# Softmax with a temperature: the first store issued ahead of two exponentials

## Chip, cores, metric

One core of one Trainium2 chip. The metric is the device time of one execution in microseconds (us); less is better.

## The reference

```python
# x: 16 x 1024 x 512, float32
x_scaled = x / 0.5
x_max = np.max(x_scaled, axis=-1, keepdims=True)
exp_x = np.exp(x_scaled - x_max)
return exp_x / np.sum(exp_x, axis=-1, keepdims=True)
```

The input is 33.55 MB and so is the output. Every byte is read once and written once.

## The kernel before

The 16,384 rows form eight tiles of 128 partitions x 16 rows x 512 elements, 4.19 MB each. Tiles 0 to 5 have a buffer of their own; tile 6 reuses tile 0's and tile 7 reuses tile 1's. SyncE issues the loads. VectorE takes the row maxima (`shift`), ScalarE the exponentials with their sums, in place. Then VectorE scales seven eighths of the rows and ScalarE the last eighth (of a block of only four rows VectorE scales all). ScalarE also issues the stores, one for each tile.

```python
    LOADS = [[(0, 4), (4, G)]] + [WHOLE] * 7
    BLOCKS = [[(0, 4), (4, 8), (8, G)]] + [WHOLE] * 6 + [[(0, 8), (8, G)]]
    STORES = [WHOLE] * 8
    BUFS = 6
    ...
    def exponentials(i):
        ...
        for g in range(hi - lo):
            row = chunks[c][:, lo + g, :]
            nc.scalar.activation(out=row, in_=row, func=EXP, bias=..., scale=2.0,
                                 accum_out=sums[i][:, g : g + 1])
    ...
    shift(0)
    shift(1)
    exponentials(0)
    for i in range(n):
        if i + 1 < n:
            exponentials(i + 1)
        scale_vector(i)
        scale_scalar(i)
        if i + 2 < n:
            shift(i + 2)
        store(i)
```

A block i is a tile or a part of one. Tile 0 is cut into blocks 0, 1 and 2, so tile 0's store comes in round i = 2, after all sixteen exponentials of block 3, which is tile 1.

## Time and profile before

| | before |
|---|---|
| time, median of the first 3 runs | 162.47 us (162.2 to 162.55) |
| span of the profiled run | 160.6 us |
| VectorE (DVE) busy | 134.6 us, 84% |
| ScalarE (ACT) busy | 102.1 us, 64% |
| bytes moved | 67.13 MB, 418 GB/s over the span |
| first store issued / landed | 45.58 / 69.3 us |
| last store issued / landed | 147.55 / 159.7 us |

The span is what the profiler sees; the time is some 1.7 us longer. A transfer has "landed" when all its bytes have arrived and those who wait for it are told. Two readings of the profile compete: that VectorE is the bound, and that the transfers (DMA) are.

This line is from the view of waits of the kernel before (engine, what it waited for, total us, times, longest):

```profile
DVE negmax L74 <- DMA xt<-in_x_dram: 9.5, 2, 4.8
```

VectorE waits for loads twice, and both times for the two pieces of tile 0. After 12.88 us it never waits for a load again.

### The profile page before, as it was taken

How to read it: one execution, taken by the hardware profiler on the slowest of the kernel's cores; microseconds unless marked ns; L12 is line 12 of the kernel's file. 1: busy time of each engine (PE TensorE's matmuls, PEld its weight loads, DVE VectorE, ACT ScalarE, POOL GpSimd, SP SyncE). 2: the span in 40 equal slices, each digit the busy share in tenths (PEclk: the TensorE clock that was granted, in tenths of full speed). 3: DMA queues.
4: the chain of work that ended last, by engine and by line, in shares of the span. 5: the costliest groups of instructions: out<-in, count | busy, mean ns of one | idle time of the engine just before them, and what ended most of it. 6: DMA issues, size and time to landing. Idle time of an engine off the chain costs nothing.

```text
span 160.6 us, 402 instructions
## 1 busy us (share of the span) xinstructions
DVE 134.6 (84%) x45; ACT 102.1 (64%) x273; POOL 0.2 (0%) x4
## 2 busy tenths in 40 slices
DVE  0507999999999999999999999999999999957000
ACT  3071549069979963998199909991899891790000
POOL 0000000000000000000000000000000000000000
DMA  5999999999999999999999999999999999999993
GB/s 182 471 400 506 400 400 498 408 392 484 424 400 384 400 457 449 400 441 465 400 424 473 408 408 492 400 392 498 416 392 490 424 392 457 457 392 449 465 392 139
DMA packets 2450, 67.13 MB, mean 418 GB/s; under 512 B 272, under 2 KB 272, under 8 KB 272
## 3 DMA queue, kind: packets, MB, share of 16 engines
q1 hardware_dynamic: 1296, 33.56, 49.3%
q10 hardware_dynamic: 1152, 33.55, 48.4%
q14 instruction: 2, 0.02, 0.0%
HBM read 33.55 MB, written 33.55 MB: 418 GB/s over the span
## 4 chain that ended last, share of the span: by engine, by line
DVE 80%; DMA 7%; ACT 4%; issue 0%; SPq 0%
DVE negmax L74 42%; DVE xt L102 36%; DMA xt<-in_x_dram 7%; ACT xt L85 4%; DVE bias L78 1%; DVE recip L100 1%; SPq L66 0%
## 5 line engine op out<-in xcount | busy, mean ns | idle before, releaser
L85 ACT ACTIVATE xt<-xt,bias 128x512 f32<-128x512 f32 x128 | 90.4, 708 | 41.7 <-DVE bias L78 41.2
L74 DVE TENSOR_REDUCE negmax<-xt 128x16 f32<-128x8192 f32 (+2 forms) x11 | 69.9, 6352 | 9.5 <-DMA xt<-in_x_dram 9.5
L102 DVE TENSOR_TENSOR xt<-xt,recip 128x7168 f32<-128x7168 f32 (+2 forms) x11 | 62.0, 5637 | 0.4
L85 ACT ACTIVATION_READ_ACCUMULATOR xt<-xt,bias 128x1 f32 x128 | 23.9, 187 | 0.0
L111 ACT ACTIVATE xt<-xt,recip 128x512 f32<-128x512 f32 x15 | 9.9, 706 | 0.0
L100 DVE RECIPROCAL recip<-sums 128x16 f32<-128x16 f32 (+2 forms) x11 | 2.4, 218 | 1.8 <-ACT xt L85 1.8
L78 DVE TENSOR_SCALAR bias<-negmax 128x16 f32<-128x16 f32 (+2 forms) x11 | 1.9, 173 | 0.4
L52 ACT ACT_TABLE_LOAD x1 | 1.3, 1283 | 0.7 <-PEq L148 0.7
L51 DVE MEMSET warm<- 128x1 f32 x1 | 0.1, 59 | 0.8 <-PEq L148 0.8
L52 ACT ACTIVATE warm<-warm 128x1 f32<-128x1 f32 x1 | 0.2, 203 | 0.0
L148 POOL MEMSET const-bfloat16-1.0<- 128x1 bf16 x1 | 0.1, 103 | 0.0
L148 POOL MEMSET const-uint8-127<- 128x1 uint8 x1 | 0.1, 103 | 0.0
L148 POOL MEMSET const-float32-1.0<- 128x1 f32 x1 | 0.1, 100 | 0.0
L148 POOL MEMSET const-float32-0.0<- 128x1 f32 x1 | 0.1, 99 | 0.2 <-issue 0.2
## 6 DMA issues: line engine op xcount, KB each, us to landing
out_dram<-xt ACTq DMA_DIRECT2D x8, 4096.0 KB, 22.8
xt<-in_x_dram SPq DMA_DIRECT2D x7, 4096.0 KB, 30.2
xt<-in_x_dram SPq DMA_DIRECT2D x1, 3072.0 KB, 11.7
xt<-in_x_dram SPq DMA_DIRECT2D x1, 1024.0 KB, 4.9
```

What stands on the lines that cost most here:

```text
L51: nc.vector.memset(warm, 0.0)
L52: nc.scalar.activation(out=warm, in_=warm, func=EXP)
L74: nc.vector.tensor_reduce(negmax[:, 0:b], chunks[c][:, lo:hi, :], axis=AX, op=MAX, negate=True)
L78: nc.vector.tensor_scalar_mul(biases[i][:, 0:b], negmax[:, 0:b], 2.0)
L85: nc.scalar.activation(out=row, in_=row, func=EXP, bias=biases[i][:, g : g + 1], scale=2.0, accum_out=sums[i][:, g : g + 1],)
L100: nc.vector.reciprocal(recips[i][:, 0:b], sums[i][:, 0:b])
L102: nc.vector.tensor_mul(rows, rows, recips[i][:, 0:k].unsqueeze(2).broadcast_to((P, k, D)))
L111: nc.scalar.activation(out=row, in_=row, func=COPY, scale=recips[i][:, g : g + 1])
L148: nc = _bacc.Bacc("TRN2", target_bir_lowering=False, num_devices=1)
```

## The change

The intent is to get the first store going sooner: two of tile 1's exponentials don't have to run before it, so they are put behind it. Nothing is added or removed.

```diff
-    def exponentials(i):
+    def exponentials(i, rows):
         c, lo, hi = blocks[i]
-        sums[i] = stats.tile([P, BMAX], fp32, name="sums")
-        for g in range(hi - lo):
+        if i not in sums:
+            sums[i] = stats.tile([P, BMAX], fp32, name="sums")
+        for g in rows:
...
-    exponentials(0)
+
+    def rows(i):
+        c, lo, hi = blocks[i]
+        cut = hi - lo - (2 if c == 1 else 0)
+        return range(cut), range(cut, hi - lo)
+
+    exponentials(0, rows(0)[0])
     for i in range(n):
         if i + 1 < n:
-            exponentials(i + 1)
+            exponentials(i + 1, rows(i + 1)[0])
         scale_vector(i)
         scale_scalar(i)
         if i + 2 < n:
             shift(i + 2)
         store(i)
+        if i + 1 < n:
+            exponentials(i + 1, rows(i + 1)[1])
```

## The prediction

> **What bounds the kernel now.** I read the page first for the busy shares, then the chain of waits, then the DMA queues, because the first two point at VectorE and the third does not.
>
> ```profile
> span 160.6 us, 402 instructions
> ...
> DVE 134.6 (84%) x45; ACT 102.1 (64%) x273; POOL 0.2 (0%) x4
> ...
> DMA  5999999999999999999999999999999999999993
> ...
> HBM read 33.55 MB, written 33.55 MB: 418 GB/s over the span
> ...
> DVE 80%; DMA 7%; ACT 4%; issue 0%; SPq 0%
> ```
>
> The chain (last line) makes VectorE the bound: it runs from one instruction to the next from 12.88 us to 147.48 us. But it ends 13 us before the span does, and what fills these 13 us is the last store. The DMA row has a 9 in every slice but the first and the last. So I cut the span into stretches to see the rate. The columns are the stretch, its length, the busy time of three engines, the clock, the DMA share and GB/s.
>
> ```profile
> 0.00:3.00 3.00, 0.06 (x1) 1.49 (x2) 0.20 (x4) 1.00 0.40 98
> 3.00:43.00 40.00, 32.37 (x15) 21.05 (x59) 0.00 (x0) 1.00 1.02 438
> 43.00:55.00 12.00, 11.93 (x5) 11.16 (x32) 0.00 (x0) 1.00 0.98 396
> 55.00:95.00 40.00, 39.86 (x9) 29.23 (x78) 0.00 (x0) 1.00 1.00 433
> 95.00:135.00 40.00, 39.79 (x13) 32.20 (x86) 0.00 (x0) 1.00 1.00 432
> ```
>
> The rate is 432 to 438 GB/s with loads alone (3 to 43 us), with loads and stores mixed (55 to 95 us) and later, when stores soon run alone. Only the stretch around the first store is lower. So the time is a sum of bytes: 67.13 MB / 433 GB/s = 155.0 us; the start costs 3 us x (1 - 98/433) = 2.3 us; the dip at the first store costs 12 us x (1 - 396/433) = 1.0 us. That is 158.3 us. The last store lands at 147.55 + 12.2 = 159.75 us (issue time and time to landing), so some 1.4 us remain for smaller losses and the confirmation of the last bytes; the span ends at 160.6 us and the time of that run was 162.34 us, 1.7 us more.
>
> Is the last store late because VectorE finished late? The store before it was issued at 133.08 us and took 17.0 us, so it landed at 150.1 us, 2.5 us after the last store was already in the queue. From landing to landing is 9.65 us, which is 4.19 MB at 434 GB/s: the queue drains at its full rate, with a backlog. VectorE and the DMA engines finish nearly together, with the DMA behind. Both need looking at.
>
> **What the Trainium skill says.** "DMA: Bandwidth & Descriptors", section "Issuing engines are not separate DMA queues": transfers started by different engines run on the same 16 DMA engines and interleave. The trace agrees: with both queues filled the sum stays at 433 GB/s. The same page, "Where 436 GB/s comes from", puts the ceiling of these 16 engines at 435 GB/s; the 432 to 438 measured here (a stretch counts whole packets, hence more than the ceiling) lies on it. "Perfetto Trace Analysis", "Identifying the Most-Contended Engine": what counts is the most contended resource, and for DMA the bandwidth reached instead of occupancy. That is why I set the rate above the chain of waits here.
>
> **The change part by part.** The compiled order of ScalarE shows one difference: the first copy (the row scaled on ScalarE) and the first store stand after 30 exponentials instead of 32, and the last two exponentials of tile 1 follow the store. The order on VectorE and SyncE is the same. Nothing is added or removed, so no byte and no instruction changes; three things move.
>
> Here is that spot in the timeline before (start, duration, instruction):
>
> ```profile
> 43.43 0.71 ACT L85 ACTIVATE xt<-xt,bias 128x512 f32<-128x512 f32 x1
> ...
> 44.14 0.71 ACT L85 ACTIVATE xt<-xt,bias 128x512 f32<-128x512 f32 x1
> 44.75 0.19 ACT L85 ACTIVATION_READ_ACCUMULATOR xt<-xt,bias 128x1 f32 x1
> 44.84 0.71 ACT L111 ACTIVATE xt<-xt,recip 128x512 f32<-128x512 f32 x1
> 45.58 0.37 ACTq L119 DMA_DIRECT2D out_dram<-xt  x1
> 46.18 0.17 DVE L78 TENSOR_SCALAR bias<-negmax 128x16 f32<-128x16 f32 x1
> 46.26 0.25 DVE L100 RECIPROCAL recip<-sums 128x16 f32<-128x16 f32 x1
> 46.39 0.72 ACT L85 ACTIVATE xt<-xt,bias 128x512 f32<-128x512 f32 x1 [0.84 <-DVE bias L78]
> ```
>
> 1. *The store.* Exponentials follow each other every 0.705 us, so two are 1.41 us. The copy starts at 43.43 and the store at 45.58 - 1.41 = 44.17 us. Nothing else holds the store back: VectorE's scaling of tile 0 ends at 37.55 us. The gain for this one store is 1.4 us at its issue.
>
> 2. *What the store feeds.* The load of tile 6 reuses tile 0's buffer and is issued when this store has landed: at 45.58 + 23.7 = 69.3 us before (SyncE issues it at 69.38 us). After, up to 1.4 us sooner. But that load takes 25.6 us and lands at 95.0 us, and VectorE only asks for tile 6 at 104.03 us. So the earlier load removes a wait that does not exist: there is no VectorE wait on a load after 12.88 us (two waits, 9.5 us in all, both on tile 0). And the DMA engines are not idle beside it either: load 5 is in flight until about 3.8 + 71.8 = 75.6 us (issue and time to landing). The store moves ahead of other bytes, and those move behind it. Loads of tiles 4 and 5 may land up to 1.4 us later; tile 5 is asked for at 87.41 us, so about 12 us are spare. Value of this part: 0.0 us.
>
> 3. *The two exponentials.* They now end after the store's issue: 44.17 + 0.37 + about 0.03 gives 44.57, the second starts at 45.27, its accumulator read ends 0.80 us later, at 46.07 us. VectorE's reciprocal needs these sums and started at 46.26 us behind its own bias instruction. So 0.2 us are spare. If ScalarE needs a few tenths more to restart after the issue than I put in, the reciprocal slips by 0.1 to 0.3 us and the whole rest of VectorE's chain with it. The next exponential waits for the bias of 46.35 us anyway, so ScalarE loses nothing.
>
> Would a slip of 0.1 to 0.3 us count? In the packet records behind the page the last store's first packet starts at 148.44 us, right when the first engine ends the store before; 15 of the 16 engines take it up between 148.4 and 148.9 us, the slowest one at 149.6 us, and it is the slowest that ends the span. A slip of up to about 1 us is hidden behind that one.
>
> Sum: store 1.4 us earlier, all hidden behind a full DMA; 0.0 to +0.1 us at the end. The span stays at 160.6 us, the time at the 162.2 to 162.55 us of before.
>
> **The rivals.**
>
> *A: the dip belongs to where the store begins.* Around the first store the rate drops to 396 GB/s, worth 1.0 us. If that came from the store meeting the load of tile 4 at a bad moment, an earlier issue could make it smaller or larger. For: it is the only place in the middle of the span where DMA time is lost. Against: the store moves by 1.4 us inside the same two queued loads (tiles 4 and 5), so the circumstances are the same; I expect the same dip 1.4 us earlier. If it vanished: 161.4 us; VectorE's chain would then be about as late as the DMA, so no more than that. If it grew by half: 162.9 us.
>
> *B: the intent comes true.* The store starts the stream of writes, and 1.4 us earlier would carry through to the end if the DMA engines were starved between 45 and 148 us: 161.0 us. Against: the share is 0.98 to 1.02 in every stretch from 3 to 135 us; a start 1.4 us sooner can't use time that is in use.
>
> *C: VectorE becomes the bound.* The late sums (part 3) push VectorE's chain. With a slip of 0.3 us the last store is issued at 147.85 us and the end is unchanged; only a slip above 1 us shows, and then by the rest. A restart cost of over 1 us on ScalarE isn't in the trace of any place. If it were: 162.7 us.
>
> **Range and chances.** The main case, no change, has about 85% and gives 162.2 to 162.6 us, the spread of the three runs before. A takes about 10%, mostly between 161.5 and 162.9 us; B and C the rest. I predict 162.4 us, and 161.9 to 162.9 us holds the main case with the milder forms of A and C. Two per cent would be 3.2 us; none of the rivals reaches it, so I put 0.98 on within 2% and 0.01 on either side.
>
> **What would show each step.** The first store should start at 44.2 us. The two exponentials behind it should begin near 44.6 us and the reciprocal of tile 1 near 46.3 us; at 46.6 us or later C is at work. The load of tile 6 should be issued 0.7 to 1.4 us before 69.38 us, and no VectorE wait on a load should be new. The rate should be 432 to 438 GB/s outside the dip, the dip again about 1 us, only sooner. The last store should land within 0.3 us of 159.75 us. I am wrong if the time leaves 161.9 to 162.9 us: below it, the dip has gone (look at the rate from 43 to 55 us) or the DMA had idle time that I did not see; above it, the last store was issued more than 1 us later, or the dip grew.

## The result

The changed kernel took 162.20 us (median of 4 runs, 162.04 to 162.22), the kernel before 162.33 us (4 runs, 162.06 to 162.55). The ratio is 0.999 with a 95% interval of 0.9972 to 1.0009: the same. A ratio here is the mean time of one kernel's runs over that of the other's of the same rounds, so it isn't quite the ratio of the medians.

First the spot that was changed, in the timeline of the kernel after (start, duration, instruction):

```profile
43.38 0.70 ACT L112 ACTIVATE xt<-xt,recip 128x512 f32<-128x512 f32 x1
44.11 0.38 ACTq L120 DMA_DIRECT2D out_dram<-xt  x1
44.53 0.72 ACT L86 ACTIVATE xt<-xt,bias 128x512 f32<-128x512 f32 x1 [0.45 <-ACT xt L112]
...
45.87 0.19 ACT L86 ACTIVATION_READ_ACCUMULATOR xt<-xt,bias 128x1 f32 x1
46.12 0.17 DVE L78 TENSOR_SCALAR bias<-negmax 128x16 f32<-128x16 f32 x1
46.20 0.24 DVE L101 RECIPROCAL recip<-sums 128x16 f32<-128x16 f32 x1
```

The store starts 1.47 us sooner than before; 0.06 us of this are of the whole trace, in which VectorE is earlier by as much. The exponentials behind it start 0.04 us after it was issued. Their sums are ready at 46.06 us, and the reciprocal still comes right behind its own bias instruction, as before. So VectorE lost nothing.

Then the load that this store sets free, in SyncE's timeline after:

```profile
68.16 0.33 SPq L66 DMA_DIRECT2D xt<-in_x_dram  x1
```

It is issued 1.22 us sooner than the 69.38 us of before. But it takes 27.7 us to land instead of 25.6, so it lands at 95.9 us, 0.9 us later than before. The store took DMA time from the loads in flight: tiles 4 and 5 land 0.9 us later too (57.2 and 76.6 us instead of 56.3 and 75.6), and tiles 6 and 7 stand behind them in the same queue. So an earlier store made every later load later. VectorE doesn't notice, since the line of the waits view is unchanged:

```profile
DVE negmax L74 <- DMA xt<-in_x_dram: 9.5, 2, 4.8
```

Last the rates, from the table of stretches after (stretch, length, busy time of three engines, clock, DMA share, GB/s):

```profile
3.00:43.00 40.00, 32.43 (x15) 21.11 (x59) 0.00 (x0) 1.00 1.01 437
43.00:55.00 12.00, 11.93 (x5) 11.27 (x32) 0.00 (x0) 1.00 0.98 396
55.00:95.00 40.00, 39.86 (x9) 29.17 (x78) 0.00 (x0) 1.00 1.00 433
95.00:135.00 40.00, 39.79 (x13) 32.20 (x86) 0.00 (x0) 1.00 1.00 433
```

They are those of before within 1 GB/s, the 396 of the dip included. The last store is issued at 147.50 us and lands 11.9 us later, at 159.4 us. That is 0.3 us sooner than before; in e11 below, the same kernel, it is 159.95 us.

### The profile page after: what moved, and what is told of

It reads as the page before. It is cut to its first block, busy times and chain, and to the rows that moved or that the text cites. A ratio compares the mean times of both kernels' runs of the same rounds, so it can differ in the third digit from the quotient of the medians.

```text
span 160.3 us, 402 instructions
## 1 busy us (share of the span) xinstructions
DVE 134.6 (84%) x45; ACT 102.2 (64%) x273; POOL 0.2 (0%) x4
## 2 busy tenths in 40 slices
DMA packets 2450, 67.13 MB, mean 419 GB/s; under 512 B 272, under 2 KB 272, under 8 KB 272
## 4 chain that ended last, share of the span: by engine, by line
DVE 80%; DMA 7%; ACT 4%; issue 0%; SPq 0%
DVE negmax L74 42%; DVE xt L103 36%; DMA xt<-in_x_dram 7%; ACT xt L86 4%; DVE bias L78 1%; DVE recip L101 1%; SPq L66 0%
```

## The experiments

My theory was: the DMA engines are full from 3 us on, so an earlier store only changes places with loads. Its rivals were that the store's start carries through to the end, that VectorE alone is the bound, and that the dip at the first store depends on where the store stands. Twelve runs were made; e11 is the changed kernel itself.

A word on one measure: most packets of 32 KB took 1213 ns in the packet records of the trace, whatever the mix of loads and stores. The dip consists of load packets that took up to 2 us (up to 3.3 us in e11). I added up what the packets took beyond that pace, for each place, as a mean over the 16 engines, in the one profiled run of each kernel:

| kernel | first store issued | excess at the first store | excess at later stores |
|---|---|---|---|
| before | 45.58 us | 0.76 us | none |
| after | 44.11 us | 0.75 us | none |
| e11, the same kernel again | 44.24 us | 1.0 us | none |
| e10, four exponentials behind | 42.70 us | 0.91 us | none |
| e12, six | 41.17 us | 0.97 us | none |
| e1, eight | 40.00 us | 1.05 us | 0.64 us |

The excess at the first store seems to rise with the shift, but this is not shown: the same kernel has 0.75 us in one run and 1.0 us in another.

### The changed kernel again, and other distances (e11, e10, e12, e1)

```diff
-        cut = hi - lo - (2 if c == 1 else 0)
+        cut = hi - lo - (4 if c == 1 else 0)   # e10; e12 has 6, e1 has 8, e11 keeps 2
```

Expected for e11:

> The changed kernel itself once more, in more rounds and on the same chip as e10. Theory 'full DMA': ratio to the kernel before 1.000 within 0.002. If the 0.13 us between the medians of the first comparison is an effect of the change, the ratio is 0.999 again with an interval that leaves 1.000 out.

Measured: 162.21 us, ratio 1.0000 (0.9988 to 1.0013). The interval holds 1.000, so no effect is shown. The medians do lie 0.10 us apart in the same direction again; so small a difference can't be told from noise here.

Expected for e1, the first of them to run:

> The changed kernel with eight exponentials of tile 1 behind the first store instead of two. The store should be issued 8 x 0.705 = 5.6 us before the 45.58 us of the kernel before, near 39.9 us, and tile 1's reciprocal stay near 46.2 us. Theory 'the 16 DMA engines are full, the store only changes places with loads': ratio 1.000 within 0.003, the dip in the rate 5.6 us sooner and still worth about 0.8 us. Rival 'the stream of writes starts sooner and carries through': 5.6 us less, ratio 0.966. Rival 'the dip belongs to the place where the store meets the loads': the dip's loss changes by half or more, time by 0.4 us or more.

Measured: 163.38 us, ratio 1.0065 (1.005 to 1.0081). The store did start 5.6 us sooner and VectorE's reciprocal did stay (46.32 us), so the rival of the carried-through start is refuted. But my own theory's 1.000 missed too: the kernel is 1.1 us slower. The same stretches of the kernel before, then of e1:

```profile
62.00:68.00 6.00, 5.93 (x4) 4.99 (x15) 0.00 (x0) 1.00 1.00 431
...
81.00:87.00 6.00, 6.00 (x1) 6.00 (x19) 0.00 (x0) 1.00 1.00 431
```

```profile
62.00:68.00 6.00, 5.93 (x4) 4.94 (x14) 0.00 (x0) 1.00 0.98 410
...
81.00:87.00 6.00, 6.00 (x1) 6.00 (x19) 0.00 (x0) 1.00 1.00 404
```

At the starts of the second and third store, near 64 and 84 us, load packets are long again, which they are not in the kernel before. With the third of these places, near 103 us, the excess is the 0.64 us of the table, and with the larger first dip some 0.9 us more than before (part of that first dip may be the scatter between runs). The last store was issued at 147.83 us and took 12.9 us, so it landed 1.0 us after the 159.7 us of before. So the sum of bytes has a second term, the pace of the packets, and this term can depend on where stores start. Two runs asked what it depends on.

e1 also shows the price that the loads pay. The load of tile 7 landed at 115.05 us before, 5.5 us ahead of VectorE; in e1 it landed at 120.81 us, and VectorE waited 0.15 us for it, too short to be counted in the view of waits. Tile 6, which the prediction looked at, had 9 us. This does not explain the 1.1 us: the last store was issued only 0.28 us later and then stood longer in the queue than before. But with a longer shift VectorE's chain would wait too.

Expected for e10:

> The changed kernel with four exponentials behind the first store: issue near 42.8 us. e1 (eight, 39.9 us) was 0.65% slower with two further stretches of long load packets, at the starts of the second and the third store. If this grows with the shift, this run loses about 0.4 us: ratio 1.002 to 1.004. If it comes only where the 16 engines start a store far apart in time (2.5 us in e1, about 1 us before), the time follows the spread at the starts of the second and third store: ratio 1.000 with a spread near 1 us, 1.004 to 1.007 with 2.4 us.

Expected for e12:

> The changed kernel with six exponentials behind the first store: issue near 41.4 us, between e10 (42.8 us, ratio 1.000) and e1 (39.9 us, ratio 1.0065). The load of tile 4 has its first packets near 41.1 us in all of them, so only e1 issues the store while tile 3 is still the one being loaded. If the loss grows with the shift: ratio 1.003 to 1.005. If it is tied to that tile boundary: ratio 1.000, within 0.002, with no long load packets at the starts of the second and third store. In both cases nothing is gained.

Measured: e10 162.26 us, ratio 0.9998 (0.9984 to 1.0011); e12 162.32 us, ratio 0.9997 (0.9983 to 1.0011). Neither has long packets at later stores. So the loss in time does not grow steadily with the shift: between 1.5 and 4.4 us early it is absent, at 5.6 us it is there. One idea fell here: that it comes when the 16 engines start a store far apart in time. In e1 they ended the first store, and so came to the second, 2.3 us apart, and 0.9 us before; but in the profiled runs of e12 and e11 they were 2.0 and 2.8 us apart, without a stretch of long packets there. The other idea is weak: in e1 alone the store is clearly issued before the packets of tile 4, which start at 41.1 us (e12's is issued at 41.17 us, on the boundary itself). One kernel on one side of a boundary is thin evidence, I have no mechanism for it, and e2 below has long packets at a later store too, though its first store comes late. This stays open.

### The first store late (e2, e3)

```diff
+        if i == 3:          # e3: i == 4
+            store(2)
-        store(i)
+        if i != 2:
+            store(i)
```

Expected for e2:

> The kernel before with the first store held back until just ahead of the second, near 59.0 us, 13.4 us late. Theory 'full DMA': six loads of 4.19 MB at 433 GB/s fill the engines from 1.8 us to about 60.5 us by themselves, so nothing idles and the time stays: ratio 1.000 within 0.005; the load of tile 6 goes out near 71 us instead of 69.4 us. Rival 'the first store's issue time carries through to the end': 13 us more, ratio 1.08.

Measured: 162.67 us, ratio 1.0022 (1.0007 to 1.0036). The time stayed within the forecast, but not the issue time, which was 54.17 us and not 59.0:

```profile
54.17 0.37 ACTq L119 DMA_DIRECT2D out_dram<-xt  x1
57.57 1.32 ACT L111 ACTIVATE xt<-xt,recip 128x512 f32<-128x512 f32 x2
58.92 0.34 ACTq L119 DMA_DIRECT2D out_dram<-xt  x1
```

The first of these stores stands behind the two copies in the program, and it was issued 3.4 us before they began. Its data had been ready since about 45.6 us, so nothing held it but the order. The Trainium skill explains this, in "Perfetto Trace Analysis", section "Sequencer Loop": the sequencer pushes engine instructions into a queue, where they wait, and executes control instructions itself. The trace agrees. The store of 58.92 us waits for the copies' results and so comes behind them. An 8.6 us later first store cost about 0.4 us, and the packet records show 0.27 us of long packets at the start of the third store.

Expected for e3:

> The kernel before with the first store held back until just ahead of the third, near 75.7 us. Theory 'full DMA': loads end near 60.5 us and the second store alone lasts to about 70.2 us, then the engines idle until the two stores of 75.7 us show packets near 76.7 us: 6.5 us lost, time 167.5 to 170.5 us, ratio 1.03 to 1.05; the load of tile 6 is issued near 87.5 us and lands some 4 us after VectorE asks for it at 104 us. Rival 'the issue time carries through': 30 us more, ratio 1.18.

Measured: 168.25 us, ratio 1.0371 (1.0358 to 1.0385). The number fits the forecast, the path to it doesn't. The store again ran ahead and was issued at 70.85 us, so the DMA engines idled for under 1 us there. The load of tile 6 still went out late, at 82.10 us, and VectorE waited for it and for tile 7:

```profile
108.15 8.69 DVE L74 TENSOR_REDUCE negmax<-xt 128x16 f32<-128x8192 f32 x1 [4.18 <-DMA xt<-in_x_dram]
...
127.53 4.42 DVE L74 TENSOR_REDUCE negmax<-xt 128x8 f32<-128x4096 f32 x1 [2.67 <-DMA xt<-in_x_dram]
...
154.53 0.34 ACTq L119 DMA_DIRECT2D out_dram<-xt  x1
```

These two waits are 6.85 us, and they move the last store from 147.55 to 154.53 us. By then the engines had run dry; this is the stretch before it, at 26 GB/s:

```profile
150.00:155.00 5.00, 4.09 (x2) 1.51 (x4) 0.00 (x0) 1.00 0.06 26
```

So a first store does set the end once it is late enough for the loads behind it to come after VectorE asks for them. In the kernel before there were 9 us to spare for tile 6 and 5.5 us for tile 7, and to be earlier than that has no value.

### Fewer bytes, and less work on VectorE (e4, e5, e6)

```diff
-    LOADS = [[(0, 4), (4, G)]] + [WHOLE] * 7                    # e4 and e6:
+    LOADS = [[(0, 4), (4, G)]] + [WHOLE] * 6 + [[(0, 8)]]       # half of tile 7 wrong on purpose
-        k = b - b // 8                                          # e5 and e6,
+        k = b - b // 4                                          # and in scale_scalar
```

Expected for e4, the half load alone:

> The kernel before with only rows 0 to 7 of tile 7 loaded (half the outputs of that tile wrong on purpose): 2.10 MB fewer bytes, all instructions on VectorE and ScalarE the same. A pure sum of bytes would give 4.8 us less, ratio 0.970. VectorE as the sole bound would give no change, 1.000. Theory 'both finish nearly together': the last store is still issued at 147.55 us and now finds idle engines, so it starts on all of them near 148.5 us and lands near 158.7 us: about 1 us less, ratio 0.992 to 0.996.

Expected for e5, the relief of VectorE alone:

> The kernel before with a quarter of each block's rows scaled on ScalarE instead of an eighth: VectorE's chain loses 6 x 1.09 + 3 x 0.56 + 2 x 0.57 = 9.4 us, and the last store is issued near 138 us instead of 147.55 us. Theory 'full DMA': no byte less, so the time stays within 1 us of 162.3 us (ratio 0.994 to 1.006). Rival 'VectorE is the bound, as the chain of waits says': 9 us less, ratio 0.942.

Expected for e6, both:

> The relief of VectorE together with the half load of tile 7 (outputs wrong on purpose). With the last store no longer late, the 2.10 MB fewer bytes should now count in full: 2.10 MB / 433 GB/s = 4.8 us less, about 157.5 us (156.8 to 158.6), ratio 0.966 to 0.977, against 0.994 with the half load alone. If the half load gained only 1 us for another reason than the late last store, this run stays near 161.2 us.

| | full load | half load |
|---|---|---|
| VectorE as before | 1 (before) | 0.994 (0.9927 to 0.9952), 161.25 us |
| VectorE relieved | 1.0018 (0.9998 to 1.0038), 162.63 us | 0.9716 (0.9695 to 0.9736), 157.70 us |

The lines of the DMA view show issue to landing of the last store, for e4, e5 and e6 in turn; the first is preceded by the stretch before that store moves in e4, the second by its issue in e5:

```profile
143.00:149.00 6.00, 4.10 (x2) 1.45 (x4) 0.00 (x0) 1.00 0.61 262
...
out_dram<-xt ACTq DMA_DIRECT2D x1, 4096.0 KB, 11.1
```

```profile
140.68 0.34 ACTq L119 DMA_DIRECT2D out_dram<-xt  x1
...
out_dram<-xt ACTq DMA_DIRECT2D x1, 4096.0 KB, 19.2
```

```profile
out_dram<-xt ACTq DMA_DIRECT2D x1, 4096.0 KB, 15.5
```

In e4 the last store is issued at 147.48 us as ever and takes 11.1 us, as little as the last store of e3: the queue ahead of it was empty. It lands at 158.6 us, 1.1 us sooner than before, and of the 4.8 us that the saved bytes are worth 3.8 us became idle time. In e5 the store is ready 6.9 us sooner, at 140.68 us, and then stands 19.2 us in the queue: nothing gained. (The forecast had 9.4 us sooner; it left out that VectorE would now wait for tile 7's load, 1.7 us, and longer for the last exponentials.) Only e6, with both, gets the bytes' worth: 162.63 - 157.70 = 4.9 us against the 2.10 MB / 433 GB/s = 4.8 us of the forecast. So the DMA rate is the bound, and VectorE's chain is a second bound only some 1 us below it. The chain of waits showed the second one.

### What the dip at the first store is (e7, e8, e9)

```diff
-    STORES = [WHOLE] * 8                                # e7
+    STORES = [[(0, 4), (4, G)]] + [WHOLE] * 7
```

```diff
+    seed = stats.tile([P, 1], fp32, name="seed", bufs=1)         # e8; e9: [P, D], scratch too
+    nc.vector.memset(seed, 0.0)
+    scratch = nc.dram_tensor("scratch", (P, 1), fp32, kind="Internal").ap()
+    nc.scalar.dma_start(out=scratch, in_=seed)
     nc.scalar.activation(out=warm, in_=warm, func=EXP)
```

Expected for e7:

> The kernel before with tile 0's store split: rows 0 to 3 of each partition go out when they are ready, near 18 us, the rest at 45.6 us as before. It asks whether the dip of 0.8 us (load packets that take up to 2 us instead of 1.213 us) belongs to the first write of the kernel or to each start of an idle store queue beside loads. First write only: one dip near 20 us, none near 48 us, time 162.3 us, ratio 1.000. Each start: two dips, time 163.1 us, ratio 1.005.

Measured: 162.13 us, ratio 0.9984 (0.9963 to 1.0006). The stretches of e7, 3 to 55 us:

```profile
15.00:27.00 12.00, 11.86 (x9) 7.66 (x21) 0.00 (x0) 1.00 0.98 393
27.00:43.00 16.00, 15.93 (x5) 10.54 (x31) 0.00 (x0) 1.00 1.00 429
43.00:55.00 12.00, 11.93 (x5) 11.16 (x32) 0.00 (x0) 1.00 1.04 441
```

The dip went with the small store of 17.79 us and left the place near 48 us. In the packet records it is 0.80 us near 20 us and 0.14 us near 49 us, and 0.24 us came near 105 us. So most of the dip comes once, with the first store, and not with each start of an idle queue.

Expected for e8:

> The kernel before with one tiny store (4 bytes from each partition) to a scratch tensor issued near 1 us, when the DMA engines have nothing to do yet. If the dip is a cost of the store queue's first use, it moves into the start and the time falls by up to 0.8 us, ratio 0.995 to 0.998. If it belongs to a start of large stores beside running loads, it stays near 48 us and the ratio is 1.000.

Measured: 168.25 us, ratio 1.0366 (1.0337 to 1.0395). The dip near 48 us is gone, as the first reading has it, but a loss of some 6 us stands at the start instead. Stretches of e8:

```profile
3.00:15.00 12.00, 2.46 (x2) 0.47 (x1) 0.00 (x0) 1.00 1.03 222
...
38.00:55.00 17.00, 16.86 (x8) 14.55 (x40) 0.00 (x0) 1.00 1.00 430
```

With 128 pieces of 4 bytes in flight, load packets took up to 6.5 us and the first load landed after 11.2 us instead of 4.9. After that, no load packet beside a store's start was long.

Expected for e9:

> As the scratch store of e8, but with 2048 bytes from each partition (0.26 MB) instead of 4. In e8 the dip at the first real store was gone and a loss of some 6 us stood at the start instead. If that loss came from the 4-byte pieces, it falls here to the usual 0.8 us or less, partly inside the 2 us in which the engines have little to do: time 161.8 to 162.9 us (0.26 MB more are 0.6 us), no dip near 48 us. If any first store that meets the very first loads is that dear, the time stays near 168 us.

Measured: 162.98 us, ratio 1.0043 (1.0029 to 1.0057). With 2048 bytes a piece the large loss was gone, which points at the 4-byte pieces meeting the first loads. (The wider memset also put the store at 1.46 us instead of 0.92 us; this was not tested apart.) The 0.26 MB more cost what they should, 0.6 us. But the dip stayed near 48 us, 0.74 us in the packet records. So "the queue's first use" is refuted as the cause: in e9 the queue had been used.

What the three runs have in common is narrower: most of the dip comes once, with the first store that meets a long queue of loads (e7 and e9), or with tiny pieces even near the first ones (e8). The packet records show two things more. The slowing begins before the store moves a byte: in the kernel before, the store is issued at 45.58 us, the long load packets begin at 47.1 us, and 29 of the 30 begin ahead of the store's first packet, at 49.65 us; in e7 all do, in e2, the least, 19 of 34. And it needs no first store: in e3 the loads start again beside running stores (issue at 82.10 us, first packet at 86.90 us), and in between 21 store packets are long, 0.95 us in the mean over the engines. Why the running queue slows in this time is not shown, and the second start of the stores in e7 (0.14 us) and the first tile's store in e8 (none) are exceptions. What happens in the engines then is open, and with it whether the 0.8 us can be had. No run beat the kernel before by more than its noise.

## Why the prediction was right

- *The bound.* Right. The sum of bytes at 433 GB/s set the time; e5 and e6 show it from both sides. That VectorE's chain ends 13 us before the span was the hint that its 80% of the chain was not the answer. Two details of the working were off. The chain is not VectorE's alone: from 137.56 to 143.33 us it runs through exponentials of ScalarE. And the 1.0 us of the dip, read from the rate of one stretch, is 0.76 us in the packet records, so the rest that the sum leaves is some 1.6 us and not 1.4.
- *The store, 1.41 us earlier.* It was 1.47 us, and 1.41 us against VectorE's instructions. Its worth was put at 0.0 us and the ratio of e11 is 1.0000.
- *What the store feeds.* Right in what counts, no new wait on a load. The load of tile 6 was issued 1.22 us sooner, in the forecast's 0.7 to 1.4. What the prediction said of tiles 4 and 5 only, that they may land later, held for tiles 6 and 7 as well (0.9 us). It looked at tile 6's spare time and not at tile 7's, which is shorter: 5.5 us before, 4.6 us after. For this change that was enough.
- *The two exponentials.* Right: the restart behind the issue took 0.04 us where 0.03 was put in, and VectorE did not slip. The margin behind it, "up to about 1 us", agrees with e4: with nothing queued ahead, the last store lands 1.1 us sooner, and this is how far the DMA bound lay above VectorE's chain. The last store landed 0.3 us sooner than before, at the edge of what the prediction allowed; e11, the same kernel, has 159.95 us, so this much is scatter.
- *Rival A.* The prediction expected the same dip 1.4 us sooner, and that is what came (396 GB/s both times). The rival's idea, that the place of the start can matter, was true further out: 0.9 us of long packets at 5.6 us early. A longer move than this change's would have left the prediction's reasoning short of a term.
- *Rivals B and C.* B is refuted by e1, C for this change by the timeline after. Note that B is no nonsense: e3 shows a late first store in the total.

## What to carry to other kernels

Before you move a transfer forward, look at the rate in stretches around it: where the engines already move as much as in any other stretch (433 GB/s here), an earlier start only exchanges one transfer for another, and the transfers that it overtakes land later. Then ask who waits for what the transfer sets free and for what it delays; here loads that were 9 and 5.5 us ahead of their reader. And a chain of waits can name the second bound: test it by relieving it alone, and together with the other one.

## What the Trainium skill lacked or had wrong

- "SBUF — State Buffer", "Summary: rules for kernel authors", says to estimate transfers between HBM and SBUF at about 358 GB/s. That would be 187.5 us for 67.13 MB; one core moved 433 GB/s here in the steady stretches and the whole kernel took 162 us. The row does not say for which case it holds, a core that streams alone, as here, or two that share the memory.
- No page that I read has the loss at the first store that meets queued loads: load packets of up to 2.0 us instead of 1.213 (3.3 in e11), 0.75 to 1.0 us in all (before, after, e11, e7, e9). Nor that packets can be long again later (0.64 us in e1, some 0.25 us in e2 and e7, 0.95 us of long store packets in e3, where loads start again).
- "DMA: Bandwidth & Descriptors", "Specifications", gives 512 bytes as the least size for full rate. It doesn't say what smaller pieces do to others: a store of 128 x 4 bytes slowed the first loads by some 6 us (e8), 128 x 2048 bytes didn't (e9).
